# Last heads' products, norm and residual in parts of 384 and 160 tokens, with the cross heads' output share as a pass of its own

## The chip, the cores and the metric

The kernel runs on one core of a Trainium2 chip. A core has TensorE (PE in the profile, for matrix products; PEld are its weight loads), VectorE (DVE), ScalarE (ACT), GpSimd (POOL) and SyncE (SP, which here starts the transfers). Each engine runs its own instructions in order and waits for the others on semaphores. The metric is device time in microseconds; before, three runs gave 810.78 at the median (809.51 to 811.42).

## The reference

One inference step of a two-layer decoder for 512 prompt tokens and 8 samples of 4 tokens, so 544 tokens of width 1024. Layer 0 is dilated attention, layer 1 is an RWKV-7 recurrence with 12 heads of 64. Both layers also attend to 256 memory tokens with 4 cross heads. The end of layer 1, which the change touches, is:

```
y, S = wkv_scan(r, decay, k, v, -kk, kk * a, s0)
mean = jnp.mean(y, axis=-1, keepdims=True)
var = jnp.mean(jnp.square(y - mean), axis=-1, keepdims=True)
y = (y - mean) * lax.rsqrt(var + GN_EPS) * ln_w.reshape(RWKV_HEADS, HEAD_DIM) + ln_b.reshape(RWKV_HEADS, HEAD_DIM)
y = y + jnp.sum(r * k * r_k, axis=-1, keepdims=True) * v
y = y.reshape(bsz, T, RWKV_W).astype(xn.dtype)
o_mem = cross_attn(q_mem, mem_kv)
h = jnp.concatenate([y, o_mem], axis=-1) * jax.nn.silu(gate)
return h @ w_out, cols[:, -1], S.astype(xn.dtype)
...
xp = xp + rms_norm(hp, norm_post[i])
xs = xs + rms_norm(hs, norm_post[i])
```

The width of h is 1024: 768 of RWKV and 256 of the cross heads. The output is y plus the residual after a norm over the 1024 columns of each token.

## The kernel before, in words

Features lie on the 128 partitions and tokens along the free axis. A row of h, called j here, is 128 features of all 544 tokens: rows 0 to 5 are two RWKV heads each, rows 6 and 7 are the cross heads. The RWKV heads are worked in three groups g of two rows, each over 8 chunks of 64 tokens of the prompt, with the 32 sample tokens apart. Group g first inverts a triangular matrix by forward substitution (`products`, lines 1449 and 1451 on VectorE, ending in the transpose at line 1459), then TensorE forms X, w, q and v for the group, and then the state goes from chunk to chunk (`recur`, lines 1675 and 1693). Two or four chunks at a time get the norm over each head (lines 1530 to 1549); when such a norm is done an event is set: norm2_4, norm2_6 and norm2_8 for the first four, the next two and the last two chunks of group 2, norm2s for its samples.

`gated(j)` makes a row of h: it loads the gate row from memory (ud), VectorE multiplies (line 1761), ScalarE rounds it to the high half (line 1762), and GpSimd, or VectorE for the rows in LOD, takes the rest as the low half (line 1763). A weight piece is split the same way (lines 304 and 305). `mm1` makes one product out of three TensorE instructions (lines 312 to 314): high by high, low weight by high, high weight by low.

`outer` works the output projection. After the gates it gates rows 6, 7, 0 and 1, waits for the end of group 1, gates rows 2 and 3, and then makes, for each of the 8 blocks mt of 128 output columns and each of two token parts (256 and 288), one sum over rows 6, 7, 0, 1, 2 and 3, which is copied to z (line 1869, VectorE for the first part, ScalarE for the second). That is 288 instructions on TensorE. Rows 4 and 5, the last heads, follow in `last(0)` (256 tokens, after norm2_4) and `last(1)` (288 tokens, after norm2_8 and norm2s): gating, 48 products each, the addition to z (line 1811), squares, their sum over the columns by TensorE (line 327), the reciprocal root (line 340 on GpSimd, cast at 347, turned by TensorE at 354), and `finish`: scaling (line 1781), adding the residual (line 1787 on GpSimd, for the first block on VectorE) and storing. Blocks of part 0 are finished between the blocks of part 1 where FIN says so; the others after it.

The order of the instructions is planned when the kernel is built. `Flow` runs all these pieces as streams that yield a cost and a delay (LAT) or the name of an event; of the streams that are ready the one with the lowest RANK goes first, and streams called dense, `outer` among them, fill in. A scheduler then places the instructions on each engine.

## Time and profile before

| what | value |
| --- | --- |
| median of three runs | 810.78 us (809.51 to 811.42) |
| the profiled execution | 809.29 us, its span 807.5 us |
| TensorE busy | 751.7 us (93%) |
| VectorE busy | 463.0 us (57%) |
| ScalarE busy | 338.6 us (42%) |
| GpSimd busy | 353.3 us (44%) |
| TensorE's mean granted clock | 0.972 |

Times in rows of the profile are from the start of the span. A timeline row gives start, duration, engine, line, operation, output <- inputs and shape, and in brackets the idle time ahead of it with what ended that. A row of a group gives the count, then after the bar the busy time and the mean of one in ns, then the idle time ahead of the group. The granted clock (PEclk) is a share of full speed. Line numbers are those of the kernel before; in the changed kernel they are 2 or 3 higher up to `gated`.

### The profile page before, as it was taken

The numbers are of one execution on the slowest core, as the hardware profiler recorded it, in microseconds if no ns is written. First come the engines' busy times: TensorE is split into PE (matmuls) and PEld (weight loads), VectorE is DVE, ScalarE is ACT, GpSimd is POOL, SyncE is SP. The second block draws the span as 40 slices with busy tenths as digits, with TensorE's granted clock in tenths as the row PEclk, the third lists the DMA queues.
The fourth block names the chain that finished last, engine by engine and source line by source line (L and its number), as shares of the span: only waits on it lengthen the run. The fifth ranks groups of instructions, "written<-read, shape, count | busy, mean of one in ns | idle before, by whom it ended". The sixth has DMA issues, their size and how long they took to land.

```text
span 807.5 us, 20072 instructions
## 1 busy us (share of the span) xinstructions
PE 751.7 (93%) x8264; PEld 637.4 (79%) x8264; DVE 463.0 (57%) x1093; ACT 338.6 (42%) x779; POOL 353.3 (44%) x390
## 2 busy tenths in 40 slices
PE   6899999999998989989999999999999999599993
PEld 5877778889874786688988889897888988389873
DVE  7733312246467455663454579854699536982375
ACT  7454321124343346535786247442365322233131
POOL 4642223323220162964543347644365444553357
PEclk9999999999999999999999999999999999689997
DMA  7464288862213574325212442200223233433003
GB/s 247 123 220 159 95 268 305 285 217 82 81 54 101 202 222 150 109 89 177 72 60 93 146 146 73 74 28 28 70 74 105 82 95 98 148 95 105 16 26 111
DMA packets 59088, 99.51 MB, mean 123 GB/s; under 512 B 6415, under 2 KB 24111, under 8 KB 58959
## 3 DMA queue, kind: packets, MB, share of 16 engines
q1 hardware_dynamic: 58996, 98.22, 37.0%
q8 instruction: 65, 1.06, 0.5%
q14 instruction: 27, 0.22, 0.1%
HBM read 84.15 MB, written 14.05 MB: 122 GB/s over the span
## 4 chain that ended last, share of the span: by engine, by line
PE 74%; DVE 13%; DMA 4%; ACT 3%; POOL 3%; issue 1%; SPq 0%; POOLq 0%; ACTq 0%; DVEq 0%
PE o L312 3%; PE o L313 2%; PE b_h L312 2%; PE o L314 2%; PE b_h L313 2%; PE b_h L314 2%; PE sc L1372 2%; PE y L1635 2%; PE z L1635 2%; PE Sx L559 2%; PE o L776 1%; PE ox L583 1%; PE pa L768 1%; PE ptx L575 1%; POOL z L1787 1%
## 5 line engine op out<-in xcount | busy, mean ns | idle before, releaser
L305 POOL TENSOR_TENSOR lo_b<-raw_b,hi_b 128x512 fp32r<-128x512 f32 x58 | 76.9, 1325 | 116.7 <-ACT hi_b L304 83.4
L305 POOL TENSOR_TENSOR lo_a<-raw_a,hi_a 128x512 fp32r<-128x512 f32 x44 | 57.2, 1301 | 138.7 <-ACT hi_a L304 111.5
L304 ACT CAST hi_a<-raw_a 128x512 fp32r<-128x512 f32 x44 | 27.3, 620 | 68.1 <-PE a15h L314 7.0
L304 ACT CAST hi_b<-raw_b 128x512 fp32r<-128x512 f32 x58 | 36.3, 626 | 41.7 <-PE b_h L314 14.1
L312 PE MATMUL b_h<-xg,hi_b 128*128 128x272 f32 x160 | 46.5, 299 | 0.6 <-DVE xv L1132 0.3
L313 PE MATMUL b_h<-xg,lo_b 128*128 128x272 f32 x160 | 46.2, 294 | 0.0
L314 PE MATMUL b_h<-xg,hi_b 128*128 128x272 f32 x160 | 45.6, 292 | 0.0
L312 PEld LDWEIGHTS b_h<-xg,hi_b 128*128 128x128 f32 x160 | 29.6, 188 | 2.9 <-issue 1.4
L1449 DVE TENSOR_TENSOR TX<-T,TT 128x30 f32<-128x30 f32 (+14 forms) x90 | 29.2, 325 | 4.1 <-ACT T L1423 2.3
L1451 DVE TENSOR_TENSOR T<-T,TX 128x30 f32<-128x30 f32 (+14 forms) x90 | 30.1, 334 | 2.3 <-DVE TX L1449 0.4
L313 PEld LDWEIGHTS b_h<-xg,lo_b 128*128 128x128 f32 x160 | 29.8, 188 | 0.3
L314 PEld LDWEIGHTS b_h<-xg,hi_b 128*128 128x128 f32 x160 | 29.7, 188 | 0.3 <-issue 0.2
L1677 POOL TENSOR_TENSOR Sd<-St,DF 128x128 f32<-128x128 f32 x21 | 8.6, 412 | 32.2 <-DVE St L1693 28.2
L753 ACT ACTIVATE P<-P,m 128x768 f32<-128x768 f32 x16 | 14.9, 935 | 16.3 <-DVE m L752 16.3
L312 PE MATMUL o<-h,hi_o1a 128*128 128x256 f32 (+1 forms) x64 | 19.2, 313 | 1.6 <-ACT h L1762 1.6
L1372 PE MATMUL sc<-AR,BK 64*64 64x128 f32 x384 | 19.2, 281 | 0.2 <-DVE bv L1318 0.2
L313 PE MATMUL o<-h,lo_o1a 128*128 128x256 f32 (+1 forms) x64 | 18.7, 305 | 0.0
L314 PE MATMUL o<-h,hi_o1a 128*128 128x256 f32 (+1 forms) x64 | 18.7, 309 | 0.0
L768 PE MATMUL pa<-ident,P 128*128 128x128 f32 x96 | 14.2, 279 | 3.5 <-DVE P L755 1.4
L768 PEld LDWEIGHTS pa<-ident,P 128*128 128x128 f32 x96 | 10.6, 142 | 6.7 <-issue 2.3
L1281 POOL TENSOR_TENSOR rv<-rv,mhalf 128x10 f32<-128x10 f32 x6 | 14.0, 2336 | 3.9 <-DVE rv L1280 3.9
L1372 PEld LDWEIGHTS sc<-AR,BK 64*64 64x64 f32 x384 | 13.4, 136 | 2.9 <-issue 0.8
(1057 smaller groups left out, 2825.0 us busy)
## 6 DMA issues: line engine op xcount, KB each, us to landing
raw_b<-in_w_in_b SPq DMA_DIRECT2D x58, 256.0 KB, 2.6
raw_a<-in_w_in_a SPq DMA_DIRECT2D x44, 256.0 KB, 2.7
kc<-in_kc SPq DMA_DIRECT2D x18, 512.0 KB, 4.7
vc<-in_vc SPq DMA_DIRECT2D x18, 512.0 KB, 5.8
out_win<-t SPq DMA_DIRECT2D x12, 272.0 KB, 2.3
PB<-bd SPq DMA_DIRECT2D x4, 576.0 KB, 7.0
x<-in_x SPq DMA_DIRECT2D x8, 272.0 KB, 6.1
xr<-in_x SPq DMA_DIRECT2D x16, 136.0 KB, 4.8
```

The source lines that it names most:

```text
L304: nc.scalar.copy(hi, raw)
L305: lo_eng.tensor_tensor(lo, raw, hi.bitcast(F32), ALU.subtract)
L312: nc.tensor.matmul(ps[:, :n], hi, xh, start=first, stop=False)
L313: nc.tensor.matmul(ps[:, :n], lo, xh, start=False, stop=False)
L314: nc.tensor.matmul(ps[:, :n], hi, xl, start=False, stop=last)
L559: nc.tensor.matmul(S[hh][64 * e:64 * e + 64, 0:256], qm[r, f, a:a + 64], kT[l][r, f, :], start=True, stop=True)
L753: nc.scalar.activation(P, P, AF.Exp, bias=m1[:, 0:1], scale=1.0, accum_out=m1[:, 1:2])
L768: nc.tensor.transpose(dst, P[:, j * 128:j * 128 + 128], ident)
L1372: nc.tensor.matmul(pts[e][unit(c, j, h)[0], a:a + 128], BK[H2[h], j, x, CH[c]], AR[H2[h], j, :, CH[c]], start=True, stop=True)
L1449: nc.vector.tensor_tensor(pd, TP[:, 0:s, s:s + 1].to_broadcast([128, s, w]), TT[:, s:s + 1, s + 1:32].to_broadcast([128, s, w]), ALU.mult)
L1451: nc.vector.tensor_tensor(TP[:, 0:s, s + 1:32], TP[:, 0:s, s + 1:32], pd, ALU.add)
L1635: nc.tensor.matmul(out, lhs, rhs, start=start, stop=stop)
```

## The change

Three things are done in `outer` and `last`, and the planner's numbers are set anew.

First, the cross heads' share (rows 6 and 7) is a pass of its own: 96 instructions over all 8 blocks, whose sums ScalarE copies to z. A second pass of 192 instructions makes the share of rows 0 to 3, and VectorE adds it to z (16 additions instead of 8 copies). Rows 6 and 7 are gated at the start, rows 0 to 3 one by one between the weight pieces, after the end of group 1. Second, the last heads' parts are LAST, 384 and 160 tokens; part 0 waits for norm2_6 too. z is laid out by row, the residual comes by four transfers at the start of part 0, and the sums of squares have a form for parts under 256. Third, GORDER, GEARLY, LAT, RANK and LOD change: the order in which the gates are made, the delays and ranks of the planner, and the rows whose low half VectorE makes.

```diff
--- before.py
+++ after.py
@@ -22,7 +22,7 @@
 TMPB = 6
 WLV = (2, 3, 4, 7)
 SQB, XNB = 9, 2
-GORDER = (6, 2, 4, 0, 7, 3, 5, 1)
+GORDER = (6, 2, 5, 4, 0, 1, 7, 3)
 COLB = 5
 HB = 3
 RAWB = 2
@@ -39,11 +39,12 @@
 LOP = (0, 3, 4)
 WOB = 10
 DU = 2
-GEARLY = 4
-LAT = [4.0, 5.82, 0.81, 0.51, 5.42, 5.2, 1.5, 0.94, 1.83, 0.6, 1.02]
-RANK = [7, 2, 7, 3, 2.5, 2.5, 3, 9]
+GEARLY = 2
+LAT = [4.0, 5.82, 0.81, 0.26, 5.42, 5.2, 1.5, 0.94, 1.83, 0.6, 0.87]
+RANK = [3.5, 2, 4, 3, 2, 2.5, 2.5, 9]
 RHO, DEBT = 0.35, 0.5
-LOD = (6, 0, 2)
+LOD = (1, 3)
+OZ = 4
 KB = 4
 CCB = 8
 PB_ = 4
@@ -53,6 +54,7 @@
 NT = 544
 HF = 272
 HALF = (slice(0, HF), slice(HF, NT))
+LAST = (slice(0, 384), slice(384, NT))
 PART = (slice(0, 256), slice(256, NT))
 SCALE = 0.125
 NEG = -1e30
@@ -322,10 +324,11 @@
 
     def add_squares(acc, sq, n, first, last):
 
-        for i in (0, 256, 128) if n > 256 else (0, 128):
+        short = n < 256
+        for i in (0, 256, 128) if n > 256 else (128, 0) if short and not first else (0, 128):
             w = min(128, n - i)
             nc.tensor.matmul(acc[0:w, i // 128:i // 128 + 1], sq[:, i:i + w], ones[:, 0:1],
-                             start=first and i == 0, stop=last and i == 128)
+                             start=first and i == 0, stop=last and i == (0 if short else 128))
 
     def rstd_begin(acc, n, name, eps=1e-6):
 
@@ -1755,47 +1758,46 @@
         if 0 in parts:
             us[j] = rw.tile([128, NT], F32, tag="u", bufs=2, name=f"ug{j}")
             nc.sync.dma_start(us[j], ud[j])
-        ts = slice(PART[parts[0]].start, PART[parts[-1]].stop)
+        ts = slice(LAST[parts[0]].start, LAST[parts[-1]].stop)
         uj = us[j][:, ts]
         if j < 6:
             nc.vector.scalar_tensor_tensor(uj, bvs[j][:, ts], vec("lnb", j), uj, ALU.add, ALU.mult)
         nc.scalar.copy(out.h1[:, 0, j, ts], uj)
         (nc.vector if j in LOD else nc.gpsimd).tensor_tensor(out.h1[:, 1, j, ts], uj, out.h1[:, 0, j, ts].bitcast(F32), ALU.subtract)
 
-    def by_row(i, tag, width, name):
-
-        n = (256, 288)[i]
-        t = rw.tile([128, width], F32, tag=tag, bufs=2, name=f"{name}{i}")
-        rows = [t[:, k * n:k * n + n] for k in range(7 + (not i))]
-        if i:
-            rows.append(tmp(f"{name}7")[:, 0:n])
-        return t, rows
+    def residual():
+
+        t = [rw.tile([128, 2048], F32, tag="SA", bufs=2, name=f"xr{k}") for k in range(2)] + [tmp("xr2")]
+        out.xr = [], []
+        for i, k, a, r0, r1 in ((0, 0, 0, 0, 5), (0, 1, 0, 5, 8), (1, 1, 1152, 0, 5), (1, 2, 0, 5, 8)):
+            n = LAST[i].stop - LAST[i].start
+            v = t[k][:, a:a + (r1 - r0) * n].rearrange("p (k t) -> p k t", t=n)
+            nc.sync.dma_start(v, x1d[:, r0:r1, LAST[i]])
+            out.xr[i].extend(v[:, r] for r in range(r1 - r0))
 
     def turn():
 
         tc.stamp_issue_order_token(flow.last(ET.DVE), "last")
 
-    def finish(i, rp, kt, xr):
-
-        z, ts = out.z[i], PART[i]
-        nc.vector.scalar_tensor_tensor(z[kt], z[kt], vec("post1", kt), rp, ALU.mult, ALU.mult)
+    def finish(i, rp, kt):
+
+        ts = LAST[i]
+        z, xr = out.z[kt][:, ts], out.xr[i][kt]
+        nc.vector.scalar_tensor_tensor(z, z, vec("post1", kt), rp, ALU.mult, ALU.mult)
         turn()
         if kt in RADD:
-            nc.vector.tensor_tensor(z[kt], z[kt], xr[kt], ALU.add)
+            nc.vector.tensor_tensor(z, z, xr, ALU.add)
             turn()
         else:
-            nc.gpsimd.tensor_tensor(z[kt], z[kt], xr[kt], ALU.add)
-        nc.sync.dma_start(O["y"][:, kt, ts], z[kt])
+            nc.gpsimd.tensor_tensor(z, z, xr, ALU.add)
+        nc.sync.dma_start(O["y"][:, kt, ts], z)
 
     def last(i, before=None):
 
-        n, ts = (256, 288)[i], PART[i]
-        z, h1 = out.z[i], out.h1
-        t, xr = by_row(i, "SA", 2048, "xr1")
-        m = 7 + (not i)
-        nc.sync.dma_start(t[:, 0:m * n].rearrange("p (k t) -> p k t", t=n), x1d[:, 0:m, ts])
-        if i:
-            nc.sync.dma_start(xr[7], x1d[:, 7, ts])
+        ts = LAST[i]
+        n, h1 = ts.stop - ts.start, out.h1
+        if not i:
+            residual()
         for j in (4, 5):
             gated(j, (i,))
         yield 0.0, 2.0
@@ -1808,67 +1810,81 @@
                 a = (mt % 2 * 2 + k) * 128
                 mm1(ps, out.w2h[:, mt // 2, a:a + 128], out.w2l[:, mt // 2, a:a + 128],
                     h1[:, 0, 4 + k, ts], h1[:, 1, 4 + k, ts], n, k == 0, k == 1)
-            nc.vector.tensor_tensor(z[mt], z[mt], ps[:, :n], ALU.add)
+            z = out.z[mt][:, ts]
+            nc.vector.tensor_tensor(z, z, ps[:, :n], ALU.add)
             turn()
             sq = tmp(f"sqo1{mt}{i}")[:, 0:n]
-            nc.scalar.activation(sq, z[mt], AF.Square)
+            nc.scalar.activation(sq, z, AF.Square)
             sqs.append(sq)
             if 0 < mt < SQ1:
                 nc.gpsimd.tensor_tensor(sqs[0], sqs[0], sq, ALU.add)
             if mt > SQ1:
                 add_squares(acc, sqs[mt - 1], n, mt == SQ1 + 1, False)
             if i and mt == 1:
-                rp0 = rstd_end(out.rvx, 256, ps_t("rs_p10"))
+                rp0 = rstd_end(out.rvx, 384, ps_t("rs_p10"))
             if mt in FIN and left:
-                finish(0, rp0, left.pop(0), out.xr)
+                finish(0, rp0, left.pop(0))
             yield 0.75, 0.2
         add_squares(acc, sqs[0], n, False, False)
         add_squares(acc, sqs[7], n, False, True)
         if not i:
-            out.rvx, out.xr = rstd_mid(rstd_begin(acc, n, "p10", 4e-6), n, "p10"), xr
+            out.rvx = rstd_mid(rstd_begin(acc, n, "p10", 4e-6), n, "p10")
             return
         rv = rstd_begin(acc, n, "p11", 4e-6)
         turn()
         rvx = rstd_mid(rv, n, "p11")
         yield 0.2, 0
         while left:
-            finish(0, rp0, left.pop(0), out.xr)
+            finish(0, rp0, left.pop(0))
         rp = rstd_end(rvx, n, zs[:, 512:1024])
         yield 0.2, 2.0
         for kt in range(8):
-            finish(1, rp, kt, xr)
+            finish(1, rp, kt)
             yield 0.0, 0.7
 
     def outer():
         yield "gates"
         out.h1 = pxg.tile([128, 2, 8, NT], F32R, tag="xg", name="h1")
-        for j in (6, 7, 0, 1, 2, 3):
-            if j == 2:
-                for e in ("end1", "norm1_8", "norm1s"):
-                    yield e
+        for j in (6, 7):
             gated(j)
             yield 0.0, 1.0
-        out.z = [by_row(i, ("AR", "BK")[i], 2176, "z1")[1] for i in range(2)]
+        for e in ("end1", "norm1_8", "norm1s"):
+            yield e
+        out.z = [t[:, NT * k:NT * k + NT] for x in ("AR", "BK")
+                 for t in (rw.tile([128, 4 * NT], F32, tag=x, bufs=2, name=f"z{x}"),) for k in range(4)]
         out.w2h = rw.tile([128, 4, 512], F32R, tag="UV", bufs=2, name="w2h")
         out.w2l = rw.tile([128, 4, 512], F32R, tag="SR", bufs=2, name="w2l")
         for m in range(4):
-            split_piece(I["w_out_b"][8 + m], f"o1c{m}", (out.w2h[:, m], out.w2l[:, m]))
             wb = split_piece(I["w_out_b"][12 + m], f"o1b{m}")
+            gated(m)
             for i in range(2):
                 mt = 2 * m + i
-                wa = split_piece(I["w_out_b"][mt], f"o1a{mt}")
                 for part in range(2):
                     n, ts = (256, 288)[part], PART[part]
-                    ps = ps_mm(f"o1{mt}{part}")
-                    for k, kt in enumerate((6, 7, 0, 1, 2, 3)):
-                        (hi, lo), a = (wb, (2 * i + k) * 128) if k < 2 else (wa, kt * 128)
-                        mm1(ps, hi[:, a:a + 128], lo[:, a:a + 128], out.h1[:, 0, kt, ts], out.h1[:, 1, kt, ts], n,
-                            k == 0, k == 5)
-                        if k % 2 and k < 5:
-                            yield 0.69, 0
-                    (nc.scalar.copy if part else nc.vector.tensor_copy)(out.z[part][mt], ps[:, :n])
+                    ps = ps_mm(f"o0{mt}{part}")
+                    for k in range(2):
+                        a = (2 * i + k) * 128
+                        mm1(ps, wb[0][:, a:a + 128], wb[1][:, a:a + 128], out.h1[:, 0, 6 + k, ts], out.h1[:, 1, 6 + k, ts], n,
+                            k == 0, k == 1)
+                    (nc.scalar.copy if part or m < OZ else nc.vector.tensor_copy)(out.z[mt][:, ts], ps[:, :n])
                     yield 0.69, 0
-        yield "norm2_4"
+        for mt in range(8):
+            if mt % 2:
+                m = mt // 2
+                split_piece(I["w_out_b"][8 + m], f"o1c{m}", (out.w2h[:, m], out.w2l[:, m]))
+            wa = split_piece(I["w_out_b"][mt], f"o1a{mt}")
+            for part in range(2):
+                n, ts = (256, 288)[part], PART[part]
+                ps = ps_mm(f"o1{mt}{part}")
+                for k in range(4):
+                    a = k * 128
+                    mm1(ps, wa[0][:, a:a + 128], wa[1][:, a:a + 128], out.h1[:, 0, k, ts], out.h1[:, 1, k, ts], n, k == 0, k == 3)
+                    if k == 1:
+                        yield 0.69, 0
+                nc.vector.tensor_tensor(out.z[mt][:, ts], out.z[mt][:, ts], ps[:, :n], ALU.add)
+                yield 0.69, 0
+        for e in ("norm2_4", "norm2_6"):
+            yield e
         yield from last(0)
         for e in ("norm2_8", "norm2s"):
             yield e
```

How this moves instructions: first on TensorE, at X21, the first product behind the inverse of group 2. Names o1 with two digits are a block and a token part of the output projection, o1b weights for rows 6 and 7, o1a for rows 0 to 3. Before:

```order
L312 MATMUL o121_9763<-h1_9443,hi_o1a2_9739 128x288
L313 MATMUL o121_9763<-h1_9443,lo_o1a2_9740 128x288
L314 MATMUL o121_9763<-h1_9443,hi_o1a2_9739 128x288
L1465 MATMUL X21_8927<-TX2_8495,SA2_7590 32x32 x32
L312 MATMUL o130_9789<-h1_9443,hi_o1b1_9733 128x256
L313 MATMUL o130_9789<-h1_9443,lo_o1b1_9734 128x256
```

In the changed kernel:

```order
L314 MATMUL o121_9868<-h1_9492,hi_o1a2_9850 128x288
L315 MATMUL o121_9868<-h1_9492,lo_o1a2_9851 128x288
L316 MATMUL o121_9868<-h1_9492,hi_o1a2_9850 128x288
L1468 MATMUL X21_8925<-TX2_8495,SA2_7590 32x32 x32
L314 MATMUL o130_9892<-h1_9492,hi_o1a3_9888 128x256
L315 MATMUL o130_9892<-h1_9492,lo_o1a3_9889 128x256
```

Three blocks stand ahead of X21 in both. Before, these are three whole blocks, 3 x 36 = 108 instructions; now the whole first pass stands there too, 96 + 3 x 24 = 168. Counted the same way, 24 and 66 stand ahead of group 1's sample norm, 187 and 239 ahead of v20, 234 and 276 ahead of the product from state 2, and all 288 ahead of the first output from state 4 in both.

Second on VectorE, at the end of the inverse. Before:

```order
L1449 TENSOR_TENSOR TX2_8495<-T2_8498,TT2_8494 128x84
L1451 TENSOR_TENSOR T2_8498<-T2_8498,TX2_8495 128x28x3
L1449 TENSOR_TENSOR TX2_8495<-T2_8498,TT2_8494 128x58
L1451 TENSOR_TENSOR T2_8498<-T2_8498,TX2_8495 128x29x2
L1449 TENSOR_TENSOR TX2_8495<-T2_8498,TT2_8494 128x30
L1451 TENSOR_TENSOR T2_8498<-T2_8498,TX2_8495 128x30
L1459 STREAM_TRANSPOSE TX2_8495<-T2_8498 128x32x32
L1869 COPY z10_9620<-o120_9743 128x256
L1466 STREAM_TRANSPOSE SA2_7590<-T2_8498 128x32x2x16
```

In the changed kernel:

```order
L1452 TENSOR_TENSOR TX2_8495<-T2_8498,TT2_8494 128x84
L1884 TENSOR_TENSOR zAR_9530<-zAR_9530,o110_9820 128x256
L1454 TENSOR_TENSOR T2_8498<-T2_8498,TX2_8495 128x28x3
L1452 TENSOR_TENSOR TX2_8495<-T2_8498,TT2_8494 128x58
L1454 TENSOR_TENSOR T2_8498<-T2_8498,TX2_8495 128x29x2
L1452 TENSOR_TENSOR TX2_8495<-T2_8498,TT2_8494 128x30
L1884 TENSOR_TENSOR zAR_9530<-zAR_9530,o111_9834 128x288
L1454 TENSOR_TENSOR T2_8498<-T2_8498,TX2_8495 128x30
L1462 STREAM_TRANSPOSE TX2_8495<-T2_8498 128x32x32
L1884 TENSOR_TENSOR zAR_9530<-zAR_9530,o120_9854 128x256
L1884 TENSOR_TENSOR zAR_9530<-zAR_9530,o121_9868 128x288
L1469 STREAM_TRANSPOSE SA2_7590<-T2_8498 128x32x2x16
```

Additions of the second pass stand between the last steps of the inverse; in all four stand between its steps, where before two copies stood, and two behind its transpose, where one copy stood.

Third on VectorE, where the last heads' rows 4 and 5 are gated for part 0 (ug4, ug5). Before, ahead of state 7 (St2_7):

```order
L1557 SCALAR_TENSOR_TENSOR bv4_7545<-gn2_4_9450,pv_76,bv4_7545 128x256
L1557 SCALAR_TENSOR_TENSOR bv5_8325<-gn2_4_9450,pv_76,bv5_8325 128x256
L1531 SCALAR_TENSOR_TENSOR yc2_6_9485<-gst2_6_9484,y2_4_9423 128x256
L1761 SCALAR_TENSOR_TENSOR ug4_10035<-bv4_7545,pv_76,ug4_10035 128x256
L1693 TENSOR_TENSOR St2_6_9502<-z2_9188,Sd2_6_9462 128x128
L1761 SCALAR_TENSOR_TENSOR ug5_10040<-bv5_8325,pv_76,ug5_10040 128x256
L1534 TENSOR_REDUCE gst2_6_9484<-y22_6_9486 128x4
```

In the changed kernel, some ten rows behind state 7:

```order
L1537 TENSOR_REDUCE gst2_8_9573<-y22_8_9575 128x4
L1537 TENSOR_REDUCE gst2s_9614<-y22s_9616 128x1
L1560 SCALAR_TENSOR_TENSOR bv4_7545<-gn2_6_9632,pv_76,bv4_7545 128x128
L1560 SCALAR_TENSOR_TENSOR bv5_8325<-gn2_6_9632,pv_76,bv5_8325 128x128
L1538 TENSOR_SCALAR gst2_8_9573<-gst2_8_9573 128x4
L1538 TENSOR_SCALAR gst2s_9614<-gst2s_9614 128x1
L1764 SCALAR_TENSOR_TENSOR ug4_10071<-bv4_7545,pv_76,ug4_10071 128x384
L1764 SCALAR_TENSOR_TENSOR ug5_10076<-bv5_8325,pv_76,ug5_10076 128x384
L1540 TENSOR_TENSOR yc2_8_9574<-yc2_8_9574,gst2_8_9573 128x256
```

The gating of part 0 moved from between the states to behind the statistics of the last two chunks' norm. The last heads' products that stood ahead of the last two chunks' norm on TensorE were 48; now they are 4.

## The prediction

> **What bounds the kernel now.** I read the chain of waits first, then stretches of 20 us, then the idle places. The page says:
>
> ```profile
> span 807.5 us, 20072 instructions
> PE 74%; DVE 13%; DMA 4%; ACT 3%; POOL 3%; issue 1%; SPq 0%; POOLq 0%; ACTq 0%; DVEq 0%
> ```
>
> TensorE carries three quarters of the chain. The profiled execution took 809.29 us, 1.8 beyond its span; the median of three runs, 810.78, is 1.5 above it. The edit touches only the end of layer 1, so only that end is read closely. Stretches, with TensorE's busy time in the second column and its granted clock behind the five engines:
>
> ```profile
> core 0: us, PE busy (x) PEld busy (x) DVE busy (x) ACT busy (x) POOL busy (x), PEclk, DMA share, GB/s
> 680.00:700.00 20.00, 15.20 (x144) 10.76 (x139) 16.33 (x43) 8.68 (x18) 10.68 (x10) 0.77 0.47 136
> 700.00:720.00 20.00, 14.97 (x122) 13.71 (x123) 18.84 (x55) 4.78 (x11) 8.47 (x8) 0.81 0.36 102
> 720.00:740.00 20.00, 20.00 (x388) 18.40 (x388) 6.67 (x11) 6.99 (x14) 7.70 (x8) 1.00 0.28 79
> 740.00:760.00 20.00, 20.00 (x352) 17.61 (x351) 4.47 (x13) 3.31 (x8) 8.13 (x10) 1.00 0.25 80
> 780.00:800.00 20.00, 14.67 (x91) 12.86 (x89) 12.43 (x32) 6.10 (x15) 14.32 (x20) 0.83 0.16 49
> ```
>
> From 680 to 720 us VectorE is the busy one (35.2 of 40 us; it runs the inverse of the last head group) and TensorE idles 9.8 us. From 720 to 760 TensorE is full and VectorE idle. The idle 9.8 us have two holes, and the waits in 685 to 712 us name who ended them:
>
> ```profile
> 690.00:692.00 2.00, 0.00 (x0) 0.00 (x0) 1.90 (x7) 0.62 (x1) 1.63 (x2) 0.67 0.82 258
> 692.00:694.00 2.00, 0.44 (x2) 0.44 (x3) 1.97 (x3) 0.65 (x1) 2.00 (x3) 0.50 0.83 274
> 702.00:704.00 2.00, 0.18 (x2) 0.00 (x0) 1.92 (x9) 0.26 (x1) 0.00 (x0) 1.00 0.71 215
> 704.00:706.00 2.00, 0.48 (x4) 0.32 (x4) 1.93 (x8) 0.00 (x0) 0.55 (x1) 0.58 0.37 126
> 706.00:708.00 2.00, 0.68 (x9) 0.58 (x10) 2.00 (x5) 0.84 (x2) 1.24 (x2) 0.50 0.00 0
> PE o L312 <- ACT h L1762: 5.2, 3, 3.6
> PE gn1s L1549 <- DVE yc1s L1537: 2.9, 1, 2.9
> ```
>
> So work that needs neither group 1 nor the inverse could run there. The marks behind it, on VectorE: the inverse's last transpose, then the states (L1695, L1693) that the chunks of group 2 hand on:
>
> ```profile
> 718.15 2.10 DVE L1459 STREAM_TRANSPOSE TX<-T 128x1024 f32<-128x1024 f32 x1
> 742.12 0.29 DVE L1695 COPY St<-z 128x128 f32<-128x128 f32 x1 [0.86 <-PE z L1635]
> 751.03 0.29 DVE L1693 TENSOR_TENSOR St<-z,Sd 128x128 f32<-128x128 f32 x1 [0.21 <-PE z L1635]
> 762.04 0.28 DVE L1693 TENSOR_TENSOR St<-z,Sd 128x128 f32<-128x128 f32 x1
> 773.30 0.28 DVE L1693 TENSOR_TENSOR St<-z,Sd 128x128 f32<-128x128 f32 x1
> ```
>
> These are states 0, 2, 4 and 7. I split the rest in three: up to that transpose, from there to state 7, and the tail of 34.2 us from state 7 to the span's end.
>
> **Up to the transpose: a slip, +1.4 (0 to +3).** In the program order 66 output products, not 24, now stand ahead of group 1's sample norm (gn1s), and 168, not 108, ahead of X21, the first product behind the transpose. Sixty products for a hole of 9.8 us, so they are covered. But VectorE is the bound there, and it gets more: before, two copies stand between the inverse's steps and ScalarE does the others; now four additions stand there, and two right behind the transpose where one copy stood.
>
> ```profile
> L1869 DVE COPY z<-o 128x256 f32<-128x256 f32 x8 | 3.4, 422 | 8.6 <-PE o L314 8.5
> L1811 DVE TENSOR_TENSOR z<-z,o 128x288 f32<-128x288 f32 x8 | 3.4, 450 | 4.6 <-PE o L314 4.6
> ```
>
> An addition of 288 costs 0.45: four of them for two copies is +0.96, and two behind the transpose for one copy +0.48. Each addition can also wait for a TensorE product with the rest of the inverse queued behind it; that is the +3. Zero is the case in which the reload of the gated rows, now spread over the weight pieces, takes as much off VectorE's queue. I take the counted instructions, +1.4.
>
> **From the transpose to state 7: -6.7 (-5 to -8).** TensorE is full there, so products that went into the hole come off. The price of one, from ten spacings of 256 columns and twenty of 288, and from two pairs at half clock:
>
> ```profile
> 779.16 0.28 PE L313 MATMUL o<-h,w2l 128*128 128x256 f32 x1
> 780.34 0.28 PE L314 MATMUL o<-h,w2h 128*128 128x256 f32 x1
> 783.81 0.68 PE L313 MATMUL o<-h,w2l 128*128 128x288 f32 x2
> 784.29 0.68 PE L314 MATMUL o<-h,w2h 128*128 128x288 f32 x2
> 787.22 0.29 PE L312 MATMUL o<-h,w2h 128*128 128x288 f32 x1
> 789.90 0.29 PE L314 MATMUL o<-h,w2h 128*128 128x288 f32 x1
> ```
>
> 1.18/10 is 0.118 us, 2.68/20 is 0.134, mean 0.126; at half clock 0.48/2 is 0.24. By the order, X21 to v20 (the group's last product ahead of its states) holds 79 before and 71 now: -1.0. From v20 to state 2's product 47 and 37: -1.3. From there to state 4's, 54 and 12: by count -5.3, but two steps cannot fall below what the chain itself needs. The steps behind state 4 hold next to no such products and took (773.30 - 762.04)/3 = 3.75 each; two at that make 7.5, against 11.0 now, so -3.5. The three last steps lose ten products of the last heads (1.2) and two gated rows on VectorE: -0.9, half of it possibly latency. Sum -6.7; by count alone it is -8, and -5 if the steps keep 4.4 each.
>
> **The tail: +4.9 (+2.5 to +8).** The first part is now 384 tokens and waits for chunk 6's norm. Before, 256 tokens' products of it ran from state 7 on, between the last chunks' work, and were over 7.3 us behind state 7. Rows of the gate, the powers and the end:
>
> ```profile
> L1761 DVE SCALAR_TENSOR_TENSOR ug<-bv,pv,ug 128x288 f32<-128x288 f32 x2 | 1.0, 544 | 0.0
> L1762 ACT CAST h<-ug 128x288 fp32r<-128x288 f32 x2 | 0.9, 432 | 0.6 <-DVE ug L1761 0.6
> L1763 POOL TENSOR_TENSOR h<-ug,h 128x288 fp32r<-128x288 f32 x2 | 1.6, 797 | 0.9 <-ACT h L1762 0.9
> 775.30 0.42 DVE L1530 TENSOR_REDUCE gst<-y 128x4 f32<-128x256 f32 x1 [0.36 <-PE y L1635]
> 775.58 0.55 POOL L1536 TENSOR_TENSOR gst2s<-gst2s,mhalf 128x1 f32<-128x1 f32 x1
> 778.64 1.02 POOL L1536 TENSOR_TENSOR gst<-gst,mhalf 128x4 f32<-128x4 f32 x1
> 792.54 2.31 PE L327 MATMUL ssz<-ones,sqo 128*128 128x1 f32 x18 [0.28 <-ACT sqo L1814]
> 795.18 0.86 POOL L340 TENSOR_TENSOR rv_p<-rv_p,mhalf 128x3 f32<-128x3 f32 x1 [1.23 <-DVE rv_p L339]
> 796.01 8.90 POOL L1787 TENSOR_TENSOR z<-z,xr 128x256 f32<-128x256 f32 x12
> ```
>
> Clock from state 7. The last norm's first reduction starts at +2.0 (775.30), and VectorE needs some 3 us for it up to the power (778.64 less 775.30 is 3.3 with other work between). Only then stand the two gated rows: 384/288 of 0.54 is 0.73 each, so +5.7 and +6.5. GpSimd does both powers (1.6) ahead of the low halves, at 384/288 of 0.80 or 1.06 each: +6.6, then +7.7 and +8.7. So TensorE has nearly nothing from +2 to +6.5, and no sum is complete before +8.7. The 48 products are 0.134 x 384/288 = 0.177 each, 8.5 us; some 10 run before +8.7, the rest needs 6.5, to +15.4 at full clock. The two holes above each halved the clock, and after the short pause ahead of the second part products still ran at half clock from 783.81 to past 784.29, at full clock by 787.22: some 3.4 us, which cost 1.7. With one such period I take +17.1; two give +18.8.
>
> The second part has 48 products of 160. Bounds: 160/256 of 0.118 is 0.074; the sum-of-squares rows send one column per product and still take 2.31/18 = 0.128. In columns 160 lies between, so 0.10. Three of eight blocks take 1.8, the first part's squares (nine products, 18 records, 2.3) follow, to +21.2; its power (0.86), a cast and hand-overs take 1.9, of which two blocks cover 1.2; transposes 0.5, three blocks 1.8, to +25.4; hand-over 0.3 and six square products 1.5 give +27.2. Before, the squares ended at 794.85, +21.55. That is +5.7. What follows is a little shorter: the additions at the end, five of 384 and seven of 160, against 8.90 for twelve of 256 and 288 (3040 columns against 3296), -0.5, and a power of two columns, not three, and smaller last parts, -0.3. So +4.9; full clock throughout gives +3.2, quicker hand-overs +2.5, both clock periods and 0.128 per product up to +8.
>
> [...]
>
> **Sum.** 1.4 - 6.7 + 4.9 = -0.4: 808.9 against the profiled execution's 809.29, or 810.4 against the median. Residual loads (four for three, idle queue), the new gate order and the ranks I cost at nothing: the first 4336 TensorE instructions stand in the same order, the gates' products have one size, and DMA is 0.16 to 0.47 busy in the long windows above. If the residual came late, the additions at the end would wait for it, one for one. I name 809.8, a little under the sum, since the middle's floor of 3.75 a step holds VectorE work that now leaves those steps.
>
> **Rivals.**
>
> Quick tail: the clock does not fall, or comes back at once, and the chunk steps go below 3.75. Then -8 + 1.4 + 3 = -3.6, so 807, down to 804 without a slip and with a step below 3.75. For it: some products of row 4 and the norm's transposes touch TensorE in the pause. Against it: the two holes above fell to 0.50.
>
> The tail decides (the slower case): the 384-token part waits behind GpSimd's powers and low halves, TensorE empties at state 7 and all 48 wide products start at half clock. Two slow periods and 0.128 for the narrow ones make the tail +7.5 to +8 against -6 and +1.5: 813.5 to 815. It decides as soon as the first complete sum comes later than 9 us behind state 7. For it: the queue order of VectorE, which puts the gated rows behind the last norm's statistics; against it: no row shows 384 columns.
>
> The hole is not filled: the early products wait for gated rows and weight halves from the same VectorE and GpSimd queues, so the slip grows to +3 and TensorE still idles. 3 for 1.4 is 1.6 more than the sum: 812, and 813 if TensorE loses time there too.
>
> [...]
>
> **How the numbers follow.** What this kernel's measurement tells from no change is about 0.2%, 1.6 us: same is 809.2 to 812.4. The near cancel, with the sum or a little under it, gets 0.42 (807 to 812.5; 0.14 of it faster, 0.24 same, 0.04 slower), the quick tail 0.27 (faster), the slow tail 0.23 (slower), the unfilled hole 0.08 (0.02 same, 0.06 slower). Faster 0.41, same 0.26, slower 0.33. The range 804 to 815 leaves out the ends of both rivals.
>
> **What would show it.** The hole: TensorE's busy time in 680 to 720 us up from 30.2 to about 37. The slip: the transpose at 718.2 plus 0 to 3. The middle: transpose to state 7 down from 55.2 to 47 to 50 us. The tail: state 7 to the end up from 34.2 to 37 to 42, with a first wide product some 6.5 behind state 7 and clock rows of 0.5 there. A transpose over 3 us late, or a tail under 36, makes the sum wrong.

## The result, and the profile after

The change is slower: 816.67 us at the median of 18 runs (807.78 to 818.8) against 810.45 for the kernel before (18 runs, 806.76 to 814.48), a ratio of 1.0070 with a 95% interval of 1.0051 to 1.0089. Three of the 18 runs took 807.8 to 811.3, at a mean granted clock of 0.971 to 0.978, and the other 15 took 814.1 to 818.8 at 0.962 to 0.972; the profile is of one of the 15 (817.75, 0.964), so it can't show why. A near cancel was forecast (809.8, range 804 to 815), so the prediction was wrong: the time lies above its range.

Stretches of the changed kernel, columns as before:

```profile
core 0: us, PE busy (x) PEld busy (x) DVE busy (x) ACT busy (x) POOL busy (x), PEclk, DMA share, GB/s
680.00:700.00 20.00, 15.71 (x157) 12.91 (x157) 16.47 (x44) 8.43 (x19) 10.69 (x11) 0.82 0.35 102
700.00:720.00 20.00, 18.38 (x149) 15.25 (x148) 17.41 (x47) 10.03 (x25) 10.79 (x10) 0.92 0.48 137
740.00:760.00 20.00, 19.52 (x454) 17.73 (x450) 6.35 (x18) 1.85 (x5) 3.61 (x6) 1.00 0.18 52
760.00:780.00 20.00, 11.74 (x203) 8.99 (x202) 12.03 (x35) 2.63 (x6) 7.82 (x10) 0.78 0.09 32
780.00:800.00 20.00, 19.60 (x112) 18.61 (x111) 10.17 (x25) 6.88 (x17) 10.34 (x13) 0.76 0.00 1
800.00:816.00 16.00, 4.88 (x25) 4.38 (x24) 7.41 (x20) 1.18 (x4) 11.87 (x17) 0.50 0.40 140
```

The hole of 680 to 720 is partly filled (34.1 us busy, 30.2 before). A new emptiness stands at 760 to 780 (11.7 us busy), where the kernel before had this row:

```profile
760.00:780.00 20.00, 18.19 (x325) 15.27 (x326) 15.17 (x44) 5.06 (x13) 9.73 (x13) 1.00 0.05 18
```

In the changed kernel the clock is mostly below 1 from there to the end. The marks on VectorE, from its timeline: first step of group 2's inverse, the transpose at its end, states 0, 2, 4 and 7 (the span is 816.0):

```profile
686.10 0.19 DVE L1452 TENSOR_TENSOR TX<-T,TT 128x30 f32<-128x30 f32 x1 [2.60 <-ACT T L1426]
723.16 2.07 DVE L1462 STREAM_TRANSPOSE TX<-T 128x1024 f32<-128x1024 f32 x1
745.49 0.29 DVE L1698 COPY St<-z 128x128 f32<-128x128 f32 x1 [0.86 <-PE z L1638]
752.82 0.29 DVE L1696 TENSOR_TENSOR St<-z,Sd 128x128 f32<-128x128 f32 x1 [1.06 <-PE z L1638]
760.47 0.28 DVE L1696 TENSOR_TENSOR St<-z,Sd 128x128 f32<-128x128 f32 x1
772.44 0.28 DVE L1696 TENSOR_TENSOR St<-z,Sd 128x128 f32<-128x128 f32 x1
```

Before, the first step was at this place:

```profile
684.29 0.19 DVE L1449 TENSOR_TENSOR TX<-T,TT 128x30 f32<-128x30 f32 x1 [0.79 <-ACT T L1423]
```

This mark moved by 1.8 us. Nearly all of that is there long before the first place where the order of the instructions differs: ScalarE's activation of the memory tokens begins at 313.39 us before and at 315.18 in the changed kernel. In the profiles of the experiments the mark lies anywhere between 682 and 695 us, so what comes ahead of it differs from execution to execution, and stages are compared from this mark on. Read in the same way from one profile each:

| kernel (passes, parts, numbers) | inverse | to state 7 | tail | sum | ratio to before |
| --- | --- | --- | --- | --- | --- |
| before (one, 256 and 288, old) | 33.9 | 55.2 | 34.2 | 123.2 | |
| the change (two, 384 and 160, new) | 37.1 | 49.3 | 43.6 | 129.9 | 1.0070 |
| two_256_new (two, 256 and 288, new) | 36.2 | 50.1 | 34.4 | 120.7 | 0.9994 |
| two_288 (two, 288 and 256, new) | 35.7 | 48.0 | 41.3 | 125.0 | 1.0052 |
| one_384_new (one, 384 and 160, new) | 36.0 | 57.1 | 41.2 | 134.2 | 1.0125 |
| two_384_old (two, 384 and 160, old) | 37.0 | 51.8 | 44.7 | 133.6 | 1.0135 |
| two_256_old (two, 256 and 288, old) | 37.1 | 54.2 | 34.4 | 125.7 | 1.0049 |

The sums are of one execution each and follow the ratios only roughly: `two_256_new` is 2.5 us shorter than before in its sum and level in its ratio. By these profiles the change gains 2.7 us up to state 7 (3.2 lost in the inverse, 5.9 won behind it) and loses 9.4 in the tail. The tail, on TensorE:

```profile
779.05 1.01 PE L314 MATMUL o<-h,w2h 128*128 128x384 f32 x2 [2.20 <-ACT h L1765]
780.86 1.01 PE L316 MATMUL o<-h,w2h 128*128 128x384 f32 x2
790.68 0.34 PE L316 MATMUL o<-h,w2h 128*128 128x384 f32 x1
792.26 0.28 PE L315 MATMUL o<-h,w2l 128*128 128x160 f32 x1
793.38 0.27 PE L316 MATMUL o<-h,w2h 128*128 128x160 f32 x1
795.98 0.41 PE L315 MATMUL o<-h,w2l 128*128 128x160 f32 x1
796.83 0.41 PE L316 MATMUL o<-h,w2h 128*128 128x160 f32 x1
797.05 0.84 PE L357 MATMUL rs_p<-ident,rvx_p 128*128 128x128 f32 x3
802.14 2.03 PE L330 MATMUL ssz<-ones,sqo 128*128 128x1 f32 x12
```

The wide part starts 6.6 us behind state 7 and ends 18.6 behind it; the narrow part and its squares are over 31.7 behind it. Before, the squares were over at 21.55. A product of 160 columns takes 1.12/10 = 0.112 at full clock (792.26 to 793.38) and 0.85/4 = 0.21 after the clock has fallen. VectorE's first additions of the wide part need its first complete sums:

```profile
783.50 1.02 DVE L1814 TENSOR_TENSOR zAR<-zAR,o 128x384 f32<-128x384 f32 x2 [1.73 <-PE o L316]
```

They waited 1.73 us for TensorE, so the first sums were complete 11.0 us behind state 7. The rows of the changed kernel's clock at this place:

```profile
776.00:780.00 4.00, 1.36 (x5) 1.15 (x6) 3.10 (x12) 1.59 (x4) 1.99 (x3) 0.77 0.01 2
780.00:784.00 4.00, 4.00 (x17) 3.34 (x15) 2.00 (x5) 0.00 (x0) 1.76 (x2) 0.50 0.00 0
784.00:788.00 4.00, 4.00 (x24) 3.88 (x23) 2.61 (x9) 2.65 (x6) 2.84 (x4) 0.88 0.00 0
```

In stretches of 1 us the clock was 1.00 up to 778, 0.57 in 778 to 779, 0.50 from 779 to 784, 0.52 in 784 to 785 and 1.00 from 785 to 788. Read as a mixture of 0.50 and 1.00, the means of the three rows make 1.8 + 4.0 + 1.0 = 6.8 us at half clock as the wide part begins.

### The profile page after: what moved, and what is told of

Its sections match the earlier page's. It is cut to its first block, busy times and chain, and to the rows that moved or that the text cites. A ratio compares the mean times of both kernels' runs of the same rounds, so it can differ in the third digit from the quotient of the medians.

```text
span 816.0 us, 20099 instructions
## 1 busy us (share of the span) xinstructions
PE 756.8 (93%) x8264; PEld 643.0 (79%) x8264; DVE 467.2 (57%) x1100; ACT 340.7 (42%) x787; POOL 353.7 (43%) x391
## 4 chain that ended last, share of the span: by engine, by line
PE 76%; DVE 12%; DMA 4%; issue 2%; POOL 2%; ACT 2%; SPq 1%; POOLq 0%; ACTq 0%; DVEq 0%
PE o L314 3%; PE o L315 2%; PE o L316 2%; PE b_h L314 2%; PE b_h L315 2%; PE sc L1375 2%; PE b_h L316 2%; PE y L1638 2%; PE o L779 2%; PE Sx L562 2%; PE z L1638 1%; DMA raw_wo<-in_w_out_a 1%; PE ssz L989 1%; PE ox L586 1%; PE pa L771 1%
## 5 line engine op out<-in xcount | busy, mean ns | idle before, releaser
L307 POOL TENSOR_TENSOR lo_a<-raw_a,hi_a 128x512 fp32r<-128x512 f32 x44 | 57.1, 1299 | 141.0 <-ACT hi_a L306 140.4
L306 ACT CAST hi_b<-raw_b 128x512 fp32r<-128x512 f32 x58 | 36.3, 626 | 41.3 <-PE b_h L316 14.1
L314 PE MATMUL o<-h,hi_o1a 128*128 128x256 f32 (+1 forms) x64 | 18.8, 299 | 0.0
L1539 POOL TENSOR_TENSOR gst<-gst,mhalf 128x8 f32<-128x8 f32 (+1 forms) x7 | 10.7, 1523 | 12.7 <-DVE gst2s L1538 7.9
L771 PEld LDWEIGHTS pa<-ident,P 128*128 128x128 f32 x96 | 10.7, 144 | 6.6 <-issue 2.4
```

The source lines that it names most:

```text
L306: nc.scalar.copy(hi, raw)
L307: lo_eng.tensor_tensor(lo, raw, hi.bitcast(F32), ALU.subtract)
L314: nc.tensor.matmul(ps[:, :n], hi, xh, start=first, stop=False)
L771: nc.tensor.transpose(dst, P[:, j * 128:j * 128 + 128], ident)
```

## The experiments

Three theories stood after the result: S, a serial chain (the wide part starts late because it needs chunk 6's norm); C, the clock (TensorE is too empty and runs at half rate); I, the inverse (VectorE's additions).

**The parts alone.** `two_256_new` puts the parts back (the residual's transfers follow the parts, in this run and in every other that changes them):

```diff
-LAST = (slice(0, 384), slice(384, NT))
+LAST = (slice(0, 256), slice(256, NT))
...
-        for e in ("norm2_4", "norm2_6"):
-            yield e
+        yield "norm2_4"
```

> The change with the parts of the last heads put back to 256 and 288 tokens (first part after norm2_4 alone), everything else as changed. Theory C (clock): from state 4 on TensorE is too empty in the changed kernel, its clock halves in the chunk steps, again behind state 7 and again under the 160-token products; with 256 and 288 the last heads' products stand between the steps again, so the clock stays at 1.00 to 780, state 4 to 7 takes at most 10 us (12.0 in the changed kernel's profile), the tail 34 to 36 and the time is 805 to 809. Theory S (serial chain): the tail is long because the wide part waits for chunk 6's norm and the powers; the same tail, but states 4 to 7 stay as they are: 808 to 811. Theory I (inverse): VectorE's additions in the inverse are the loss; the time stays above 812.

It gave 809.63, ratio 0.9994 (0.9970 to 1.0018): with the two passes and the new numbers kept, the whole loss is in the parts. State 7 was at 775.39, and the first products of the last heads ran ahead of it:

```profile
771.01 0.50 PE L314 MATMUL o<-h,w2h 128*128 128x256 f32 x2
775.39 0.27 DVE L1696 TENSOR_TENSOR St<-z,Sd 128x128 f32<-128x128 f32 x1
794.80 2.33 PE L330 MATMUL ssz<-ones,sqo 128*128 128x1 f32 x18 [0.28 <-ACT sqo L1817]
```

The last squares end 21.7 behind state 7, as before, and the clock was 1.00 from 772 to 796. But states 4 to 7 took 12.8 us (762.61 to 775.39), not the 10 that C expected, and the clock fell among them here too (0.71 in 764 to 768, 0.86 in 768 to 772). So the steps did not get faster with the products back in them.

**Late or narrow.** `two_288` has parts of 288 and 256 tokens: no narrow part, but the first one reaches into chunk 4 and must wait like the 384.

```diff
-LAST = (slice(0, 384), slice(384, NT))
+LAST = (slice(0, 288), slice(288, NT))
...
```

> The change with parts of 288 and 256 tokens: nearly the sizes of before, but the first part now reaches 32 tokens into chunk 4 and so needs chunk 6's norm, as the 384-token part does. Theory S (late start): the first product of the part comes 6 to 7 us behind state 7 and the tail is 40 to 44, the time 814 to 818, though no part is narrow. Theory N (narrow second part: 160 columns cost as much as a weight load and keep the clock low): the tail is 35 to 38 and the time 809 to 812.

813.93, ratio 1.0052 (1.0027 to 1.0078), tail 41.3:

```profile
777.41 0.28 DVE L1696 TENSOR_TENSOR St<-z,Sd 128x128 f32<-128x128 f32 x1
782.93 0.85 PE L314 MATMUL o<-h,w2h 128*128 128x288 f32 x2 [2.02 <-ACT h L1765]
803.67 2.72 PE L330 MATMUL ssz<-ones,sqo 128*128 128x1 f32 x12
```

The first product comes 5.5 behind state 7 and the squares end 29.0 behind it. With 32 tokens more in the first part the tail grows by 6.9 over `two_256_new`; 384 and 160 add 2.3 to that. (This profile ran at a granted clock of 0.95 where TensorE was full, so its 41.3 is if anything a little long.) The ratios split the same way: 0.58% for the 32 tokens, 0.18% for the rest. S is shown for the larger share, together with the half clock that came with the late start: 0.77 in 780 to 784, 0.50 in 784 to 788 and 0.81 in 788 to 792. This run does not part the two. The narrow part's own share in the ratios, 1.0070 against 1.0052, is inside the intervals.

**The clock, twice.** `warm` adds needless products where TensorE is empty. For that, part 0 also waits for the event at the end of group 2 (end2):

```diff
+    def warm(n, name, c):
+        pw_ = ps_mm(f"warm{name}")
+        for _ in range(n):
+            nc.tensor.matmul(pw_[:, 0:128], ident, kept[2, c].rearrange("p j t -> p (j t)"), start=True, stop=True)
...
-        for e in ("norm2_4", "norm2_6"):
+        for e in ("norm2_4", "norm2_6", "end2"):
...
+        warm(4, 0, 4)
+        warm(4, 1, 5)
+        warm(4, 2, 6)
+        warm(14, 9, 7)
```

> The change, and 26 needless TensorE products of 128 columns (ident by a state): four behind each of states 4, 5 and 6 and fourteen behind state 7, whose sums nobody reads. Theory C: the clock stays at 1.00 from 760 to at least 785, states 4 to 7 take 8 to 10 us instead of 12, the products of 384 run at 0.17 from the first on, and the time falls by 3 to 8, to 808 to 813, though work is added. Theory S: nothing is gained, the products lie in the way: 816 to 820.

The same stretches of the changed kernel first, then of `warm`:

```profile
764.00:768.00 4.00, 2.30 (x52) 1.68 (x51) 3.11 (x8) 0.42 (x1) 1.36 (x3) 0.99 0.00 0
768.00:772.00 4.00, 3.34 (x40) 2.19 (x35) 1.49 (x4) 0.00 (x0) 2.09 (x3) 0.50 0.17 66
772.00:776.00 4.00, 2.87 (x61) 2.38 (x57) 1.43 (x5) 0.00 (x0) 0.00 (x0) 0.66 0.25 86
```

```profile
764.00:768.00 4.00, 4.00 (x66) 2.61 (x64) 2.43 (x8) 0.42 (x1) 1.91 (x3) 1.00 0.00 0
768.00:772.00 4.00, 3.94 (x85) 2.94 (x82) 1.75 (x5) 0.00 (x0) 0.50 (x1) 1.00 0.41 152
772.00:776.00 4.00, 3.25 (x30) 3.06 (x28) 2.39 (x12) 0.56 (x2) 1.53 (x2) 1.00 0.00 0
```

The clock stayed up through the steps, as meant (1.00 from 764 to 776), though it still fell behind 776 (0.73 in 776 to 780). States 4 to 7 took 12.6 us all the same (757.40 to 769.99; 12.0 in the change), with twelve needless products among them. The time did not follow either: 815.17, ratio 1.0065 (1.0034 to 1.0096), tail 42.9.

In the profile of `warm` the clock was 1.00 from 784 to 796 and 0.79 from 796 to 800, under the same second part of 160 columns. Its first and last product, the transposes of the first part's reciprocal root with the product behind them, and VectorE at that place:

```profile
788.53 0.24 PE L314 MATMUL o<-h,w2h 128*128 128x160 f32 x1
794.88 0.55 PE L357 MATMUL rs_p<-ident,rvx_p 128*128 128x128 f32 x3 [0.20 <-ACT rvx_p L350]
797.03 0.35 PE L314 MATMUL o<-h,w2h 128*128 128x160 f32 x1 [1.60 <-DVE zBK L1822]
798.32 0.40 PE L316 MATMUL o<-h,w2h 128*128 128x160 f32 x1
795.53 0.61 DVE L1794 SCALAR_TENSOR_TENSOR zAR<-zAR,pv,rs_p 128x384 f32<-128x384 f32 x1 [1.83 <-PE rs_p L357]
796.18 0.56 DVE L1797 TENSOR_TENSOR zAR<-zAR,xr 128x384 f32<-128x384 f32 x1
796.66 0.54 DVE L1822 TENSOR_TENSOR zBK<-zBK,o 128x160 f32<-128x160 f32 x2
```

From the end of the wide part (788.70) to the end of its last product this second part took 10.0 us, where the changed kernel's took 11.3. For 1.60 us TensorE stood still behind the transposes: its next product waits for an addition of VectorE (L1822), and VectorE first does the scaling (L1794) that needs the transposes and a residual addition (L1797).

`wide` takes the narrow part's products over 320 columns and uses the last 160:

```diff
-                    h1[:, 0, 4 + k, ts], h1[:, 1, 4 + k, ts], n, k == 0, k == 1)
+                    h1[:, 0, 4 + k, NT - 320:NT] if i else h1[:, 0, 4 + k, ts], h1[:, 1, 4 + k, NT - 320:NT] if i else h1[:, 1, 4 + k, ts], 320 if i else n, k == 0, k == 1)
...
-            nc.vector.tensor_tensor(z, z, ps[:, :n], ALU.add)
+            nc.vector.tensor_tensor(z, z, ps[:, 320 - n:320] if i else ps[:, :n], ALU.add)
```

> The change with the second part's 48 products taken over 320 columns (tokens 224 to 543) and the last 160 columns of each sum used: needless work, the result is the same. Theory C (clock): the clock doesn't fall under the second part, which then takes 9 to 10 us from its first to its last product, not 11.3 as in the changed kernel's profile, and the time falls by 1 to 3. Theory S (chain): the products get 0.143 instead of 0.112 at full clock, nothing is won: within 1 of the changed kernel or 1 to 3 slower.

The changed kernel under its narrow part, then `wide` under its second part:

```profile
792.00:796.00 4.00, 4.00 (x35) 4.00 (x34) 0.81 (x4) 1.12 (x4) 1.84 (x3) 0.90 0.02 4
796.00:800.00 4.00, 3.60 (x17) 3.38 (x17) 2.29 (x6) 1.22 (x4) 0.59 (x2) 0.50 0.01 2
```

```profile
788.00:792.00 4.00, 4.00 (x32) 4.00 (x32) 0.81 (x3) 0.81 (x3) 1.10 (x2) 1.00 0.01 4
792.00:796.00 4.00, 2.39 (x17) 2.15 (x16) 1.79 (x5) 0.95 (x3) 1.34 (x3) 1.00 0.01 2
```

With more columns per product the clock was 1.00 in each 4 us from 784 to 800, where the changed kernel's fell to 0.50. Yet the second part took 11.3 us (786.75 to 798.10), as in the change: its wider products cost more (0.148 each at full clock, from 792.12 to 793.75, against 0.112), and TensorE then waits 1.69 us for an addition of VectorE (2.39 of 4 busy). The ratio is 1.0069 (1.0044 to 1.0093); its tail of 42.3 is 1.3 shorter. So C holds in this much: the clock was 1.00 under the added work of both runs where the changed kernel's was 0.50. But that won 0.7 and 1.3 us of the tail in these profiles, and nothing that the ratios show (1.0065 and 1.0069 against 1.0070). What the clock alone is worth in the tail no run shows: both runs add work, and in both the wide part still met a slow stretch (a clock of 0.73 in `warm` and 0.61 in `wide` from 776 to 780).

**The additions.** `noadd` replaces the second pass's additions by copies on ScalarE.

```diff
-                nc.vector.tensor_tensor(out.z[mt][:, ts], out.z[mt][:, ts], ps[:, :n], ALU.add)
+                nc.scalar.copy(out.z[mt][:, ts], ps[:, :n])
```

> The changed kernel with the 16 additions of the second pass replaced by copies on ScalarE. Left out: the cross heads' share is overwritten, so the output lacks it. It prices the additions alone. Theory I (additions lengthen the inverse): four additions of 0.44 and their waits of 1.1 for TensorE go, the inverse takes 34 to 34.5 instead of 37.1, and the time falls by 2 to 3, to 813 to 815. If the gated rows and the norm of group 1 on VectorE are the cause, the inverse stays at 36 to 37 and the time within 1.5 of the changed kernel.

```profile
684.90 0.19 DVE L1452 TENSOR_TENSOR TX<-T,TT 128x30 f32<-128x30 f32 x1 [2.60 <-ACT T L1426]
719.18 2.03 DVE L1462 STREAM_TRANSPOSE TX<-T 128x1024 f32<-128x1024 f32 x1
772.48 0.28 DVE L1696 TENSOR_TENSOR St<-z,Sd 128x128 f32<-128x128 f32 x1
```

The inverse took 34.3, 2.8 less with the additions and their waits gone. But the way to state 7 then took 53.3 instead of 49.3, and the ratio stayed at 1.0077 (1.0054 to 1.0101). Theory I falls: from the inverse's first step to state 7 it is 87.6 without the additions and 86.3 with them. Why the second stretch takes back more than it was given stays open.

**The other two edits.** `one_384_new` makes one pass again (rows 6, 7, 0 to 3 in one sum, copies to z), `two_384_old` and `two_256_old` have the planner's numbers of before, and `two_256_gord` of these only the gate order, GEARLY and LOD.

```diff
-        for m in range(4):
-            wb = split_piece(I["w_out_b"][12 + m], f"o1b{m}")
-            gated(m)
...
+                    for k, kt in enumerate((6, 7, 0, 1, 2, 3)):
...
+                    (nc.scalar.copy if part else nc.vector.tensor_copy)(out.z[mt][:, ts], ps[:, :n])
```

> The change with the output products of rows 6, 7, 0 to 3 in one pass again (copies to z, no additions), parts 384 and 160 and the new numbers kept. Theory I: the inverse is 33.9 long as before, not 37, and the time falls by 3 or more, to 811 to 813. Theory C: 60 products come back into the full stretch, the steps to state 4 cost 5 to 6 more, the tail's clock still falls behind state 7: 815 to 820. Theory S: like C for the tail, 815 to 820.

```diff
-GORDER = (6, 2, 5, 4, 0, 1, 7, 3)
+GORDER = (6, 2, 4, 0, 7, 3, 5, 1)
...
-GEARLY = 2
-LAT = [4.0, 5.82, 0.81, 0.26, 5.42, 5.2, 1.5, 0.94, 1.83, 0.6, 0.87]
-RANK = [3.5, 2, 4, 3, 2, 2.5, 2.5, 9]
+GEARLY = 4
+LAT = [4.0, 5.82, 0.81, 0.51, 5.42, 5.2, 1.5, 0.94, 1.83, 0.6, 1.02]
+RANK = [7, 2, 7, 3, 2.5, 2.5, 3, 9]
...
-LOD = (1, 3)
+LOD = (6, 0, 2)
```

> The change with the planner's numbers of before (gate order, delays, ranks, rows whose low half VectorE makes); two passes and parts 384 and 160 kept. Theories C, S and I put the loss into the passes and parts: within 3 us of the changed kernel, 813 to 819. If the numbers are what costs, it comes to 811 or less.

> Two passes with parts 256 and 288 and the planner's numbers of before: the pass alone. If the passes are the gain and the numbers do nothing: as with the new numbers, 808 to 811, with the stretch from transpose to state 7 at 49 to 52 and the tail at 34 to 35. If the numbers of before cost what they cost with 384 and 160 (5.8), 814 to 817.

> Two passes and parts 256 and 288 with the new delays and ranks, but the gate order and the rows with low halves on VectorE of before. The two sets of numbers differ by 3 us (812.6 and 809.6). If delays and ranks carry this, 809 to 811; if the gate order and the low halves do, 812 to 814.

`one_384_new` gave 821.32 (1.0125, 1.0091 to 1.0158), above every time that was expected: with the new numbers and parts the second pass is a gain of about 0.5%, as the 57.1 against 49.3 to state 7 says. Its inverse was 36.0 without any addition, not the 33.9 of theory I. `two_384_old` gave 822.51 (1.0135, 1.0110 to 1.0160), above both times that were expected, and `two_256_old` 812.59 (1.0049, 1.0029 to 1.0069), between the two: the new numbers are worth about 0.6% with either parts, and two passes with the old numbers are slower than the kernel before. `two_256_gord` lies between at 811.42 (1.0004, 0.9978 to 1.0030), beside 0.9994 with all new numbers, so delays and ranks carry most of it.

`two_256_lod` moves the low halves of rows 1 and 3 from VectorE to GpSimd:

```diff
-LOD = (1, 3)
+LOD = ()
```

> Two passes, parts 256 and 288, new numbers, and the low halves of rows 1 and 3 on GpSimd, not VectorE. Theory I (the inverse is lengthened by what VectorE does between its steps): two low halves of 0.79 go, the inverse is 34.5 to 35 instead of 36.2, the time falls by 1 to 2, to 807 to 809. Against it: GpSimd delivers the low halves later, TensorE waits, the inverse waits for the sums: no gain.

The ratio is 1.0048 (1.0025 to 1.0071) against 0.9994 with these low halves on VectorE: slower, so theory I's expectation failed here too.

**A better version.** The last residual additions set the end in both kernels. `two_256_radd` is `two_256_new` with one addition more of each part on VectorE; `before_radd` is the same edit on the kernel before.

```diff
-RADD = (0,)
+RADD = (0, 4)
```

> Two passes, parts 256 and 288, new numbers, and one more residual addition of each part on VectorE (blocks 0 and 4, not 0 alone): the best version so far with GpSimd's last additions cut from 12 to 10 of 0.75 each. If those additions set the end, as the chain of before shows, the tail falls by 1 to 1.5 from 34.4 and the time to 808 to 809; if VectorE's scalings set it, nothing or a loss of up to 1.

> The kernel before with the residual additions of blocks 0 and 4 on VectorE, not of block 0 alone. If the 0.5% of the version with two passes, 256 and 288 tokens and this edit comes from the edit, this kernel gains the same, a ratio of 0.994 to 0.998; if it comes from the two passes, nothing: 0.998 to 1.002.

`two_256_radd` gave 807.79, ratio 0.9954 (0.9924 to 0.9985): faster than both kernels. `before_radd` gave 808.17, ratio 0.9987 (0.9969 to 1.0005). The intervals overlap, so how much of the gain needs the two passes stays open. Nor does the profile of `two_256_radd` explain it: its tail is 35.4, not shorter; in that of `before_radd` it is 33.4, 0.8 shorter.

## Why the prediction was wrong, point by point

- **The hole is filled: right in part.** TensorE's busy time in 680 to 720 rose from 30.2 to 34.1, not to 37.
- **The slip, +1.4 (0 to +3): measured +3.2.** In the inverse four additions of 0.438 took 0.9 us more than the two copies of before, as counted. They also waited 1.1 us for TensorE's sums:

```profile
DVE zAR L1884 <- PE o L316: 1.1, 4, 0.3
```

That is 2.0 of the 3.2; the other 1.2 stays open.

- **The middle, -6.7 (-5 to -8): measured -5.9, near in part by luck.** States 0 and 2 came 3.2 sooner where the counts said 2.3 (22.3 and 7.3 us against 24.0 and 8.9). State 4 came 7.7 behind state 2, where 7.5 was put and 11.0 had been. States 4 to 7, put at -0.9, took 12.0 against 11.3. `two_288`, which differs only behind them, shows why: there they took 10.7, near the 10.4 that was put. The first two steps take the same in both; the last took 3.64 (773.77 to 777.41) at a clock of 0.95, and 4.93 in the change (767.51 to 772.44), where the clock was 0.50 from 768 to 772.
- **The tail, +4.9 (+2.5 to +8): measured +9.4. This is the term that failed.** Its start held: the first wide product was put at +6.5 and came at +6.6, and the first product with a low half came at +8.4 (780.86), 0.7 behind the +7.7 put for that low half. The first complete sum, put behind +8.7, came only at +11.0, with these products at half clock. The end of the wide part was put at +17.1, with one slow period, and came at +18.6: the half clock lasted 6.8 us, twice the 3.4 of the prediction's one period; for two it had +18.8. The second part with the first part's squares was put at 8.3 us, to +25.4, and took 11.3, to +29.9. Behind the last squares 11.9 us were put and 11.8 measured. The step that failed most is thus the second part, 3.0 of the 4.5 us. One cause is the clock: "0.10" per product was 0.112 at full clock and 0.21 at half, and over half of the time ran at half clock (0.60 in 795 to 796, 0.50 from 796 on). In `warm`, nearly all at full clock (1.00 from 788 to 796, 0.79 in 796 to 800), the same part took 10.0, so by these two profiles the clock was some 1.3 of the 3.0. The other 1.7 is mostly a wait that the sum did not have: behind the transposes TensorE's sums wait for VectorE's scaling and residual addition (1.60 in `warm`). In the changed kernel only 0.40 of it shows (ahead of 799.49), with its products at half clock (0.50 in 796 to 800).
- **The planner's numbers, put at nothing,** were worth about 0.6%, a gain. Part of it is in the counts of the middle, which were taken from the order that these numbers make.
- **The rivals.** The slow tail, at 0.23, named the mechanism that decided (the wide part behind chunk 6's norm), and put it at 813.5 to 815. Its point of decision, a first complete sum later than 9 us behind state 7, was passed at 11.0. So this rival was right in its mechanism, and short by 1.4 us in the tail at its largest. The quick tail did not occur. Of the unfilled hole the slip of 3 came (3.2), with 3.9 of the 9.8 us filled. That two passes lose with the numbers of before (1.0049 in `two_256_old`) was no rival of mine.

## What to carry to other kernels

Before making an early part of a tail larger, look at which event it must then wait for: 32 tokens beyond such a boundary cost 6.9 us of the tail here, three quarters of what 128 cost (0.58% of 0.76% in the ratios), since all of the part's work moves behind the last state. When two parts share one engine, count also the first part's reduction and its round trip over other engines inside the second part's time; in the two runs here a clock kept up by extra work did not shorten the time (ratios of 1.0065 and 1.0069 against 1.0070).

## What the runs showed that I had not expected

The clock fell while TensorE had no idle time: the changed kernel's TensorE was busy 4.00 of 4 us from 792 to 796 and the granted clock averaged 0.90 there (1.00 up to 795, 0.60 behind it), then 0.50, under products of 160 columns and sums of one column; with 320 columns in their place (`wide`) it was 1.00 from 784 to 800. Narrow work alone does not explain the fall: in `warm` the same products and sums ran from 788.5 to 794.4 with the clock at 1.00. What brought it down stays open. At full clock a product of 160 columns took 0.112 us against 0.118 for one of 256, and twelve of a single column took 1.30 (793.49 to 794.79 in the changed kernel), 0.108 each, so the narrow part saved next to nothing per product.
